# Softmax scaled behind the product with v, weight blocks rounded on ScalarE, and a q held as a rounded pair in a hybrid attention / DeltaNet / RG-LRU trunk

## The chip, the cores and the metric

One core of a Trainium2 chip runs the whole kernel. TensorE (PE; its weight loads are shown as PEld), VectorE (DVE), ScalarE (ACT), GpSimd (POOL) and the DMA queues of SyncE (SP) each run their own list of instructions in order and wait for one another by semaphores. The metric is the device time of one execution in microseconds; three runs gave 2277.67, 2280.9 and 2282.2 us (median 2280.9).

## What is computed

Two layers over 1024 tokens of width 1024, float32. Layer 0 projects x into two head groups: (A) sliding-window attention, 8 query heads on 2 key/value heads of 64, window 128, rotary positions, a learned sink per head; (B) four gated DeltaNet heads of 128. An output projection joins them. Layer 1 is a Griffin recurrent block. Each mixer is followed by a layer norm on `alpha*x + mixer(x)`, then a squared-ReLU MLP of width 4096 and a second layer norm. What the change touches is the attention:

```python
s = jnp.einsum('bnqhgd,bnkhd->bnhgqk', qb, kb) * (DH ** -0.5)      # masked to the window
p = jax.nn.softmax(jnp.concatenate([s, sink], axis=-1), axis=-1)[..., :-1]
o = jnp.einsum('bnhgqk,bnkhd->bnqhgd', p, vb)
```

Dividing each row of exp(s - max) by its sum before the product with v, or dividing the row of the product by it, gives the same o.

## The kernel before

**Halves and streams.** The tokens are cut into two halves of 512 (c = 0 and c = 1). Each half has a stream, a Python generator that runs its projections, MLPs and recurrent blocks: long rows of 128x512 matmuls, "dense work". Beside them run mixers, generators with small steps that wait for other engines: the four attention blocks of a half (`attention`, one `attn_block` per 128 tokens), what goes ahead of them (`attn_preps`: rotary positions, transposes of k and q), the DeltaNet heads (`head_mid`) and the layer norms. State is carried from the first half to the second.

**The order on TensorE.** The order is written while the program is built. `Clock` is a model of the engines; the loop at the end of `trunk` takes a mixer's next step when the model says that its inputs are there, and a step of a stream otherwise, the first half's before the second's while both are in the same phase, the second's first once the first is in its MLP. Each TensorE instruction is tied behind the one before, so that on the chip TensorE follows this order whatever happens. A stream that lacks a resource yields `BLOCK`, and the other is tried. A `UNIT` is the end of a piece, where the loop may change streams.

**Granules and rings.** Large tiles come from a pool of 14 granules of 128x2048 floats (ring "g"), counted by hand: `need("g", n)` blocks a stream until n are free, `gran()` takes one, `free` gives it back. A half's activations (`ActT`) take four: two quads of rows, each as a rounded high part h and the rest l. The attention slots of both halves take two (`slots(8)`: eight tiles of 128x512, `tl`), the residual rows of a mixer's output (`yg` in `mix_out`) two, and `q_proj` one (`st["qg"]`, the projected q of a half, given back when all four `attn_prep` have read it) beside the first quad of the output `oT`. Smaller rings t, s and f hold 128x512 tiles.

**Products in three passes.** Float32 products are made of rounded fp32r parts: `mm3` issues h*h, h*l and l*h. A weight block of 128x1024 is loaded on SP's queue into one of three `ws` buffers (`wblock`); `split` rounds it into `wh`, on VectorE for every fifth block (`HV`) and on ScalarE otherwise, and VectorE subtracts to make `wl`; there are three of each. A block feeds 24 matmuls. Small float32 matmuls are issued directly and show as two records each in the trace, transposes as one.

**The second half's way.** `hybrid(1, ...)` projects one head's k, q and v (`head_front`), the attention's k and v (`kv_proj`), then q (`q`, with `need("g", 3)`), spawns its attention and goes on with the heads; the projection of head 0's z (`head_z`) waits until the first half's `mix_out` has claimed the tiles of its layer norm, and for two granules. The first half's `mix_out` needs two granules before its output projection (`hout`, eight weight blocks) can start, then four for the transposed norm, which it takes over from `oT`.

**Seven products for eight.** Once the second half has made its layer's output projection, a first half's MLP goes over, at an even eighth of the hidden width, from `straight` to `seven`, a Strassen form with 7 products of 24 matmuls in place of 8 per quarter of the second weight matrix.

**An attention block.** `attn_block` makes scores for four pairs of heads (`mx`, from `kT` and qT), masks them and takes the row maximum on VectorE, makes exponentials and row sums `den` on ScalarE, multiplies each of eight 128x256 tiles by its head's 1/den on ScalarE, transposes them on TensorE, copies them from PSUM (VectorE and ScalarE in turn), multiplies by v (`vraw`) into the bank `po`, and splits the result into oT.

Of the kernel before, what the change touches and what calls it, by code (L numbers as in the profile page):

```python
# [17 lines left out]
P = 128  # L18
# [6 lines left out]
GB = 14  # L25
HP = 50
MARGIN = 0.5
WB, WS, HV = 3, 3, 5
RINGS = dict(t=11, s=10, f=4)
FW = 528  # L30
LN_EPS = 1e-5
# [182 lines left out]
def trunk(ctx: ExitStack, tc, I, out):  # L214
# [34 lines left out]
    def gran(dt=F32):  # L249
        return take("g", gpool.tile([P, 2048], dt, tag="g", name=nm("g")))  # L250
# [87 lines left out]
    V.tensor_scalar(rcn, rcs, 4.0, None, ALU.mult)  # L338
    V.tensor_scalar(rcs, rcs, -4.0, None, ALU.mult)

    wcount = [0]

    def split(h, l, x):

        wcount[0] += 1
        (V.tensor_copy if wcount[0] % HV == 0 else S.copy)(h, x)
        V.tensor_tensor(l, x, h, ALU.subtract)

    def wblock(src, n=1024, hl=None):
# [409 lines left out]

    def q_proj(c, x, st, oT):  # L760
        ps = yield from proj_tm([I["hin_q"][i] for i in range(4)], x, 512)
        st["qg"] = gran()
        for n in range(NT):
            oT.quad(0, n)
            S.copy(st["qg"][:, n * CH:(n + 1) * CH], ps[n])
        yield UNIT

    def kv_proj(c, x, st, oT, pre):
        ps = yield from proj_tm([I["hin_kv"][i] for i in range(4)], x, 264, pre=pre)
# [24 lines left out]
        V.tensor_tensor(x4[:, :, :, 1, :], a4[:, :, :, 1, :], b4[:, :, :, 0, :], ALU.add)  # L794

    def attn_prep(c, n, st, tl, o):
        q, kr = v4(st["qg"][:, n * CH:(n + 1) * CH]), st["k"][n]
        yield from need("f", 2)
        a, b, qs = tl[n % 2], ts("f"), v4(ts("f"))
        rope(kr.unsqueeze(1), kr.unsqueeze(1), 1, n, a[:, :128], b[:, :128])  # L800
        rope(qs, q, 4, n, a, b)
        yield at(kr, qs)
        ps = mx_ps()
        PE.transpose(ps[:, :P], kr, ident)
        kT = cpool.tile([P, P], F32, tag="kT", name=nm("kT"), bufs=4)
        V.tensor_copy(kT, ps[:, :P])
        ps = mx_ps()
        for g in range(4):
            PE.transpose(ps[:, g * P:(g + 1) * P], qs[:, g, :], ident)
        free("f", b, qs)  # L810
        S.copy(a, ps)
        o["qT"], o["kT"] = a, kT
        yield at(a, kT)
        o["ok"] = True

    def attn_block(c, n, st, oT, tl, o):
# [34 lines left out]
        S.activation(es, es, AF.Exp)  # L851
        V.tensor_tensor(den, den, es, ALU.add)
        V.reciprocal(den, den)
        for m in (0, 2, 1, 3):
            for g2 in range(2):
                i = 2 * (2 * (m // 2) + g2) + m % 2
                S.activation(pm[m][:, g2, :w], pm[m][:, g2, :w], AF.Copy, scale=den[:, i:i + 1])
        yield at(*pm)
        po = mx_ps()
        pend = None  # L860
# [12 lines left out]
        yield lambda: 0.0  # L873


# [345 lines left out]
    def attn_preps(c, st, o):  # L1221
# [6 lines left out]
        free("g", st["qg"])  # L1228

    def attention(c, st, oT, o):  # L1230
        for n in range(NT):
# [14 lines left out]
    def hybrid(c, x, oT, st, rs):  # L1246
# [21 lines left out]
        for h in range(4):  # L1268
# [235 lines left out]
```

## Time and profile before

| | |
|---|---|
| runs | 2277.67, 2280.9, 2282.2 us; median 2280.9 |
| the profiled execution | 2280.57 us, its span 2278.7 us (1.9 us lie around the span) |
| TensorE busy | 2216.7 us (97%) in 12436 matmuls |
| VectorE, ScalarE busy | 1545.9 us (68%), 1049.1 us (46%) |
| mean granted TensorE clock | 0.991 |

A row of instructions gives line, engine, operation, output <- inputs by the names of the tiles with their numbers left out, shape and count; then busy time and the mean ns of one; then the idle time ahead of them and what ended it. Nearly all rows bear line 178 or 206, the helpers that record every operation, so tiles tell the work apart: `mm` and `mx` are PSUM banks, `g` granules, `wh`, `wl` and `ws` weight blocks, `asc` the small tile with den, `vraw`, `kT`, `kraw` the attention's v and k, `csb` constants with the identity (a matmul from it is a transpose), `S` the DeltaNet state. Matmul ends are modelled: a matmul's own duration is longer than the distance to the next start, so costs are best taken from start to start.

### The profile page before, as it was taken

Reading aid. Unit: us, or ns where it says so; the run is one execution under the profiler, and the core shown is the slowest. Engines: PE = TensorE matmul, PEld = TensorE weight load, DVE = VectorE, ACT = ScalarE, POOL = GpSimd, SP = SyncE. Lnnn points to the kernel's source line nnn. Section 1 sums busy time; section 2 is a strip of 40 time slices with the busy share of each in tenths; the row PEclk is TensorE's granted clock in tenths of the full one; section 3 lists DMA queues with packets and bytes.
Section 4 is the critical chain, followed back from the end, with each engine's and each line's share of the span. In section 5 each row is a group of like instructions: output and inputs, shape, how many; then the busy total and the mean of one; then the engine's idle time right before and its main releaser. Section 6 shows DMA issues by size and latency. Waiting matters only on the chain.

```text
span 2278.7 us, 31897 instructions
## 1 busy us (share of the span) xinstructions
PE 2216.7 (97%) x12436; PEld 1790.4 (79%) x12436; DVE 1545.9 (68%) x2809; ACT 1049.1 (46%) x1874; POOL 28.9 (1%) x56
## 2 busy tenths in 40 slices
PE   8999989999999999999999999999999999999997
PEld 7767866778878887888888878878788887888886
DVE  7787684766645666596567898685565656776477
ACT  5465444434332344454344577373434444444442
POOL 0000000000000000000000000000000000000000
PEclk9999999999999999999999999999999999999999
DMA  4121221266778666677764343322533443454341
GB/s 165 61 78 39 94 67 45 74 175 178 216 213 225 196 211 200 210 241 229 226 216 149 128 138 105 136 79 97 180 107 121 139 148 123 155 166 148 120 163 69
DMA packets 87064, 332.22 MB, mean 146 GB/s; under 512 B 9600, under 2 KB 9984, under 8 KB 78720
## 3 DMA queue, kind: packets, MB, share of 16 engines
q1 hardware_dynamic: 73808, 275.32, 35.2%
q0 software_dynamic: 4608, 33.56, 7.8%
q10 hardware_dynamic: 8496, 21.30, 2.7%
q8 instruction: 97, 1.59, 0.3%
q14 instruction: 55, 0.45, 0.1%
HBM read 321.75 MB, written 75.50 MB: 174 GB/s over the span
## 4 chain that ended last, share of the span: by engine, by line
PE 85%; DVE 9%; ACT 3%; DMA 1%; issue 1%; ACTq 0%; DVEq 0%; SPq 0%
PE mm L206 66%; PE mx L206 17%; DVE g L178 3%; DVE wl L178 2%; PE mx L210 2%; DVE s L178 1%; DMA ws<-w 1%; ACT g L178 1%; ACT wh L178 1%; ACT s L178 1%; DVE t L178 1%; DVE f L178 1%; ACT f L178 0%; ACT t L178 0%; DVE lnw L178 0%
## 5 line engine op out<-in xcount | busy, mean ns | idle before, releaser
L206 PE MATMUL mm<-g,wh 128*128 128x512 f32 x2816 | 883.7, 395 | 3.6 <-DVE g L178 3.0
L178 DVE TENSOR_TENSOR wl<-ws,wh 128x1024 fp32r<-128x1024 f32 (+1 forms) x444 | 538.3, 1212 | 396.1 <-ACT wh L178 391.8
L178 ACT CAST wh<-ws 128x1024 fp32r<-128x1024 f32 (+1 forms) x356 | 371.5, 1044 | 705.8 <-PE mm L206 605.3
L206 PEld LDWEIGHTS mm<-g,wh 128*128 128x128 f32 x2816 | 521.6, 188 | 113.4 <-DVE g L178 5.1
L206 PE MATMUL mm<-g,wl 128*128 128x512 f32 x1408 | 549.5, 390 | 0.5 <-DVE wl L178 0.5
L206 PE MATMUL mm<-wh,s 128*128 128x512 f32 x1152 | 376.6, 393 | 0.7 <-DVE g L178 0.7
L206 PEld LDWEIGHTS mm<-g,wl 128*128 128x128 f32 x1408 | 264.7, 188 | 57.0 <-DVE wl L178 1.0
L206 PEld LDWEIGHTS mm<-wh,s 128*128 128x128 f32 x1152 | 216.3, 188 | 46.7 <-ACT s L178 1.1
L206 PE MATMUL mm<-wh,g 128*128 128x512 f32 (+1 forms) x768 | 239.3, 383 | 6.6 <-ACT wh L178 6.4
L206 PE MATMUL mm<-wl,s 128*128 128x512 f32 x576 | 224.3, 389 | 0.0
L206 PE MATMUL mx<-wh,s 128*128 128x512 f32 x576 | 187.8, 392 | 1.2 <-DVE s L178 1.2
L206 PEld LDWEIGHTS mm<-wh,g 128*128 128x128 f32 x768 | 143.0, 191 | 33.8 <-ACT wh L178 6.4
L178 ACT CAST s<-g 128x512 fp32r<-128x512 f32 x172 | 104.7, 622 | 105.2 <-PE mm L206 53.7
L178 DVE TENSOR_TENSOR s<-g,s 128x512 fp32r<-128x512 f32 x172 | 116.1, 685 | 44.7 <-ACT s L178 44.7
L206 PE MATMUL mm<-wl,g 128*128 128x512 f32 (+1 forms) x384 | 144.1, 375 | 0.2 <-DVE wl L178 0.2
L206 PEld LDWEIGHTS mx<-wh,s 128*128 128x128 f32 x576 | 108.1, 188 | 24.1 <-DVE s L178 2.0
L206 PEld LDWEIGHTS mm<-wl,s 128*128 128x128 f32 x576 | 108.3, 188 | 20.9
L206 PE MATMUL mx<-wl,s 128*128 128x512 f32 x288 | 112.1, 389 | 0.0
L178 DVE CAST wh<-ws 128x1024 fp32r<-128x1024 f32 x88 | 60.4, 686 | 73.0 <-PE mm L206 66.3
L178 DVE TENSOR_TENSOR g<-g,mm 128x512 f32<-128x512 f32 x136 | 89.1, 682 | 14.6 <-PE mm L206 14.2
L178 ACT ACTIVATE g<-mm 128x512 f32<-128x512 f32 x100 | 59.3, 593 | 73.0 <-PE mm L206 73.0
L206 PEld LDWEIGHTS mm<-wl,g 128*128 128x128 f32 x384 | 73.3, 191 | 11.7 <-DVE wl L178 0.6
(231 smaller groups left out, 2401.3 us busy)
## 6 DMA issues: line engine op xcount, KB each, us to landing
ws<-w SPq DMA_DIRECT2D x232, 512.0 KB, 3.3
ws<-t SPq DMA_DIRECT2D x96, 512.0 KB, 3.3
t<-w POOLq DMA_DIRECT2D x32, 1024.0 KB, 9.1
ws<-hin_fm SPq DMA_DIRECT2D x32, 512.0 KB, 3.3
t<-w SPq DMA_DIRECT2D x16, 1024.0 KB, 6.7
t<-t SPq DMA_DIRECT2D x16, 1024.0 KB, 6.5
ws<-rin SPq DMA_DIRECT2D x32, 512.0 KB, 3.3
ws<-hout SPq DMA_DIRECT2D x16, 512.0 KB, 3.4
```

Of the source, the lines that this page charges most:

```text
L178: r = f(*a, **k)
L206: ins = self.pe.matmul(out, lhsT, rhs, start=start, stop=stop, skip_group_check=fresh)
L210: return self._pe(self.pe.transpose(out, x, ident), out, [x], 0.00042 * 2 * out.shape[-1])
```

## The change

Four things. (1) `split` rounds every weight block on ScalarE. (2) In `attn_block` the eight multiplications by 1/den go. Behind the product with v, den (128x8) is transposed on TensorE, copied to `dT` (8x128) by ScalarE, and spread by eight float32 matmuls, each with one column of the identity, repeated 64 times, as the stationary operand, into a 128x512 bank; ScalarE copies that bank to the slot tile `tl[4]`, VectorE multiplies by `po`, and the split into oT reads the slot tile. All copies of transposed scores out of PSUM are made by ScalarE. (3) For the second half, `q_proj` splits q into the parts h and l of oT's first quad and takes no granule of its own; `attn_prep` adds the two parts. `q` then asks for two granules. (4) The `UNIT` at the end of `q_proj` goes, and one is added after a head's `head_mid` is spawned.

```diff
     def split(h, l, x):
-        wcount[0] += 1
-        (V.tensor_copy if wcount[0] % HV == 0 else S.copy)(h, x)
+        S.copy(h, x)
         V.tensor_tensor(l, x, h, ALU.subtract)
...
     def q_proj(c, x, st, oT):
         ps = yield from proj_tm([I["hin_q"][i] for i in range(4)], x, 512)
-        st["qg"] = gran()
+        g = st["qg"] = gran() if c == 0 else None
+        st["q"] = []
         for n in range(NT):
-            oT.quad(0, n)
-            S.copy(st["qg"][:, n * CH:(n + 1) * CH], ps[n])
-        yield UNIT
+            h, l = oT.quad(0, n)
+            if g is None:
+                split_ps(h, l, v4(ps[n]))
+                st["q"].append((h, l))
+            else:
+                S.copy(g[:, n * CH:(n + 1) * CH], ps[n])
+                st["q"].append(v4(g[:, n * CH:(n + 1) * CH]))
...
     def attn_prep(c, n, st, tl, o):
...
         rope(kr.unsqueeze(1), kr.unsqueeze(1), 1, n, a[:, :128], b[:, :128])
+        if c:
+            V.tensor_tensor(qs, *q, ALU.add)
+            q = qs
         rope(qs, q, 4, n, a, b)
...
         V.reciprocal(den, den)
-        for m in (0, 2, 1, 3):
-            for g2 in range(2):
-                i = 2 * (2 * (m // 2) + g2) + m % 2
-                S.activation(pm[m][:, g2, :w], pm[m][:, g2, :w], AF.Copy, scale=den[:, i:i + 1])
         yield at(*pm)
         po = mx_ps()
...
-                (S.copy if h else V.tensor_copy)(pT, ps)
+                S.copy(pT, ps)
                 yield at(pT)
                 PE.matmul(po[h * 64:(h + 1) * 64, :], vv[:, h * 64:(h + 1) * 64], pT, start=(i == 0),
                           stop=(i == len(keys) - 1))
+        yield at(den)
+        ps = mx_ps()
+        PE.transpose(ps[:8, :P], den, ident)
+        dT = cpool.tile([8, P], F32, tag="dT", name=nm("dT"))
+        S.copy(dT, ps[:8, :P])
+        yield at(dT)
+        ps = mx_ps()
+        for i in range(8):
+            g, h = divmod(i, 2)
+            PE.matmul(ps[h * 64:(h + 1) * 64, g * P:(g + 1) * P], ident[0:8, i:i + 1].to_broadcast([8, 64]), dT,
+                      start=True, stop=True)
+        S.copy(tl[4], ps)
+        V.tensor_tensor(tl[4], po, tl[4], ALU.mult)
         h, l = oT.quad(0, n)
-        split_ps(h, l, v4(po))
+        S.copy(h, v4(tl[4]))
+        V.tensor_tensor(l, v4(tl[4]), h, ALU.subtract)
...
         def q():
-            yield from need("g", 3)
+            yield from need("g", 3 - c)
...
             spawn(head_mid(c, h, st, d[h], oT, rs[h % len(rs)]))
+            yield UNIT
```

More of the change, by code (lines that the diff above doesn't have):

```diff
@@ L27 @@
 MARGIN = 0.5
-WB, WS, HV = 3, 3, 5
+WB, WS = 3, 3
 RINGS = dict(t=11, s=10, f=4)
@@ L339, in trunk @@
     V.tensor_scalar(rcs, rcs, -4.0, None, ALU.mult)
-    wcount = [0]
     def split(h, l, x):
-        wcount[0] += 1
-        (V.tensor_copy if wcount[0] % HV == 0 else S.copy)(h, x)
+        S.copy(h, x)
         V.tensor_tensor(l, x, h, ALU.subtract)
@@ L796, in attn_prep @@
     def attn_prep(c, n, st, tl, o):
-        q, kr = v4(st["qg"][:, n * CH:(n + 1) * CH]), st["k"][n]
+        q, kr = st["q"][n], st["k"][n]
         yield from need("f", 2)
@@ L853, in attn_block @@
         V.reciprocal(den, den)
-        for m in (0, 2, 1, 3):
-            for g2 in range(2):
-                i = 2 * (2 * (m // 2) + g2) + m % 2
-                S.activation(pm[m][:, g2, :w], pm[m][:, g2, :w], AF.Copy, scale=den[:, i:i + 1])
         yield at(*pm)
         po = mx_ps()
-        pend = None
         for i, (_, vv) in enumerate(keys):
@@ L1227, in attn_preps @@
             yield from attn_prep(c, n, st, slot["tl"], o[n])
-        free("g", st["qg"])
+        if c == 0:
+            free("g", st["qg"])
     def attention(c, st, oT, o):
```

## The prediction

> **What bounds the kernel now.** I read the page first, then windows, then TensorE's timeline where the windows show it idle. The page says that TensorE is busy 97% of the span. A dense stretch of the chain of waits gives its price: 480 matmuls of 128x512 in 108.94 us, 0.227 us from start to start. Windows (columns: us, then busy us and instruction counts of PE, PEld, DVE, ACT, POOL; granted clock; DMA share; GB/s) show where it isn't full.
>
> ```profile
> PE 2216.7 (97%) x12436; PEld 1790.4 (79%) x12436; DVE 1545.9 (68%) x2809; ACT 1049.1 (46%) x1874; POOL 28.9 (1%) x56
> ...
> 702.00 108.94 PE mm L206 x480
> ...
> 150.00:200.00 50.00, 44.44 (x267) 33.27 (x266) 42.04 (x115) 33.30 (x103) 0.30 (x3) 1.00 0.25 75
> 260.00:317.00 57.00, 55.97 (x399) 46.09 (x401) 46.40 (x158) 29.30 (x98) 0.00 (x0) 1.00 0.26 84
> 317.00:367.00 50.00, 39.05 (x409) 24.02 (x395) 28.31 (x94) 22.75 (x64) 0.00 (x0) 0.80 0.16 54
> 367.00:420.00 53.00, 53.00 (x252) 37.31 (x251) 23.41 (x61) 24.05 (x64) 0.00 (x0) 1.00 0.18 60
> 420.00:470.00 50.00, 46.09 (x219) 37.15 (x220) 47.93 (x117) 26.14 (x58) 0.53 (x1) 0.93 0.27 95
> 1300.00:1450.00 150.00, 147.82 (x658) 121.27 (x657) 131.39 (x205) 101.70 (x157) 0.30 (x3) 0.99 0.40 135
> 1450.00:1600.00 150.00, 144.63 (x644) 118.64 (x643) 100.67 (x157) 79.22 (x116) 0.00 (x0) 0.99 0.27 90
> ```
>
> One stretch stands out: from 317 to 367 us the granted clock is 0.80 and no engine is near full. The timeline of TensorE shows why; the row of SP's queue is from the timeline of all engines.
>
> ```profile
> 316.47 0.39 PE L206 MATMUL mm<-g,wl 128*128 128x512 f32 x1
> 316.79 0.45 PE L206 MATMUL mx<-t 32*32 32x32 f32 x32
> ...
> 356.57 1.07 PE L206 MATMUL mx<-g,vraw 128*64 128x512 f32 x2 [0.41 <-DVE g L178]
> 357.57 0.66 PE L210 MATMUL mx<-csb,g 128*128 128x128 f32 x4
> 358.06 0.61 PE L206 MATMUL mx<-S,t 128*128 128x128 f32 x4
> ...
> 360.54 1.16 PE L206 MATMUL mx<-kT,g 64*128 64x128 f32 x16
> 361.63 0.33 PE L210 MATMUL mx<-csb,kraw 128*128 128x128 f32 x1
> 362.01 0.66 PE L210 MATMUL mx<-csb,f 128*128 128x128 f32 x4
> ...
> 364.96 0.48 PE L206 MATMUL mm<-wh,g 128*128 128x512 f32 x1
> ...
> 371.90 0.39 PE L206 MATMUL mm<-wh,g 128*128 128x512 f32 x1
> 372.13 0.60 PE L206 MATMUL mx<-t,t 128*128 128x128 f32 x4
> 372.49 0.48 PE L206 MATMUL mm<-wh,g 128*128 128x512 f32 x1
> ...
> 306.00 67.64 SPq L178 DMA_DIRECT2D ws<-hout  x4
> ```
>
> Between 316.7 (316.47 + 0.227) and 364.96 us there is no dense matmul at all, only steps of the second half's attention and its first DeltaNet head: a hole of 48.3 us. Dense work is at hand: the loads of `hout`, the first half's output projection, start at 306.00, and that projection starts at 364.96, right behind the transposes of the second half's fourth `attn_prep` (361.63 and 362.01). That is where `qg` is given back. Counting granules in the code at the start of the hole: the first half's oT 4, slots 2, the second half's x 4, its qg 1, its first quad of oT 2. That makes 13 of 14; one is free, and `mix_out` asks for two.
>
> **The change part by part.**
>
> *q in two parts.* Without qg, 12 granules are taken and two are free when the first half's `mix_out` asks. It then starts its output projection before the second half's `head_front` for head 1, which has the dense work up to 316.47. Eight blocks of 24 matmuls (8 x 24 x 0.227 = 43.6 us) become filler for the attention, with their eight loads on SP's queue ahead of three loads of `hin_fm`, and the residual loads on ACT's queue earlier; DMA is busy 0.16 in the hole, so I charge nothing for them; uncovered, one costs the 3.4 us of this row of the page once. The hole's small work must still run. The other groups are of the window 317 to 367:
>
> ```profile
> ws<-hout SPq DMA_DIRECT2D x16, 512.0 KB, 3.4
> ...
> L206 PE MATMUL mx<-g,vraw 128*64 128x512 f32 x16 | 11.3, 794 | 2.6 <-DVE g L178 2.5 <-ACT g L178 0.2
> L210 PE MATMUL mx<-csb,g 128*128 128x128 f32 x32 | 7.2, 349 | 0.9 <-ACT g L178 0.9
> L206 PE MATMUL mx<-kT,g 64*128 64x128 f32 x64 | 4.9, 285 | 0.0
> L206 PE MATMUL mx<-t,t 128*128 128x128 f32 x18 | 4.1, 348 | 1.4 <-DVE t L178 1.3
> L206 PE MATMUL mx<-S,t 128*128 128x128 f32 x16 | 3.6, 364 | 0.0
> L206 PE MATMUL mx<-t 32*32 32x32 f32 x208 | 3.5, 200 | 3.3 <-DVE t L178 2.7 <-DVE kraw L178 0.6
> L206 PE MATMUL mx<-t,t 64*64 64x64 f32 x16 | 2.2, 316 | 2.6 <-DVE asc L178 2.1 <-DVE t L178 0.5
> ```
>
> From start to start in undisturbed places: two `vraw` records 1.00 us (356.57 to 357.57), so 8.0 for 16; four `csb,g` 0.49 (to 358.06), 3.9 for 32; sixteen `kT,g` 1.09 (360.54 to 361.63), 4.4 for 64; four `t,t` between dense matmuls 0.36 (372.13 to 372.49), so 0.09 a record and 3.1 for 34 of `t,t` and `S,t`; the 32x32 groups 0.45 per 32, 2.9; the 64x64 group 2.2 as recorded; two lots of `csb,kraw` and `csb,f` at 0.38 + 0.66, 2.1. Together 26.6 us, some 27. Filling the hole is worth 48.3 - 27 = **21 us**. A part of that comes back: the layer norm now runs earlier, beside two attention blocks, and VectorE is already busy 47.93 of 50 us in its present window, 420 to 470. Dense cover left for it is head 1's `head_front` alone (72 matmuls, 16 us), since `head_z` must wait for the slots' two granules, to the end of the attention. Present waits are these:
>
> ```profile
> 461.92 1.71 PE L210 MATMUL mx<-csb,g 128*128 128x128 f32 x8 [2.25 <-DVE g L178]
> ...
> 465.77 0.79 PE L206 MATMUL mm<-g,wh 128*128 128x512 f32 x1 [1.67 <-DVE g L178]
> ```
>
> 2.25 + 1.67, 4 us. I double them: **+4**, between 0 and the whole 21 (a rival below). The second half's q costs VectorE four subtractions out of PSUM and four additions at 0.68 us, 5.5 us between 230 and 365; it has 10.6 idle us in 260 to 317 alone, and nothing waits on these but the preparation of a block two ahead.
>
> *Softmax behind the product.* These rows bear on it, the first from the timeline of all engines, the others from the groups of the whole span:
>
> ```profile
> 315.36 3.29 ACT L178 ACTIVATE g<-g,asc 128x256 f32<-128x256 f32 x8
> ...
> L178 ACT COPY g<-mx 128x512 f32<-128x512 f32 x23 | 13.5, 586 | 44.0 <-PE mx L210 44.0
> L178 DVE COPY g<-mx 128x512 f32<-128x512 f32 x15 | 10.3, 689 | 16.9 <-PE mx L210 16.9
> L178 DVE TENSOR_TENSOR g<-g,mx 128x512 f32<-128x512 f32 x64 | 41.8, 681 | 0.2 <-PE mx L206 0.2
> ```
>
> 3.29 us a block leave ScalarE, ahead of the transposes. Added per block on TensorE: a transpose (0.38) and 16 records of 128 columns. No row has this shape. Paired like `kT,g` the 16 cost 1.09; at 0.09 each 1.44; at the 0.15 of the isolated `S,t` row (0.61 / 4) 2.4. I take 1.44, the row between dense matmuls, with 0.08 for the re-entry (1.9 in all; bounds 1.2 and 2.8). Four blocks of the second half now lie among dense work and pay in full, 7.6 us. The first half's four lie in stretches like 150 to 200, where TensorE idles 5.6 of 50 us for VectorE: they fall in part into such waits, but TensorE's order is fixed and a wait is filled only by what stands behind it: I charge a quarter, 1.9. Together **+9.5**, between 4.8 (the second half's at 1.2) and 22 (eight at 2.8).
>
> The Trainium skill (TensorE: Matmul & The Clock Gate, Part 3: Packing small matmuls) says that matmuls whose outputs lie in different column groups of the array run side by side, 2.38 times as fast for three. The two heads of a pair write partitions 0 to 63 and 64 to 127, so by it the 16 records would cost about half of 1.44 as an estimate, and the sum would be some 4 us lower; no row here has such a pair back to back, so that stays unshown.
>
> The rest of the tail (a copy of 0.59, the product of 0.68, the split) follows behind TensorE's last step of a block: the next block's scores don't wait for it, and it costs only a longer hold of the bank `po`, one of four. The chain of a block gives up 3.29 us and takes TensorE's 1.8 and the copy to dT, at most 0.59: even. VectorE loses 15 copies (10.3 us) and takes eight products (5.4), ScalarE takes the copies at 0.59: nothing on TensorE's path.
>
> *Rounding on ScalarE.*
>
> ```profile
> L178 ACT CAST wh<-ws 128x1024 fp32r<-128x1024 f32 x349 | 367.1, 1052 | 696.8 <-PE mm L206 596.7 <-PE mx L206 28.7 <-DMA ws<-w 27.6
> L178 DVE CAST wh<-ws 128x1024 fp32r<-128x1024 f32 x87 | 60.0, 689 | 71.9 <-PE mm L206 65.3 <-PE mx L206 4.6 <-DMA ws<-t 1.9
> ```
>
> 87 casts of 0.689 leave VectorE, and as many of 1.052 come to ScalarE: -60 and +92 us. A block feeds 5.4 us of TensorE and three are buffered, so 0.36 us more ahead of `wl` is hidden by two blocks' matmuls. Casts wait for a `wh` buffer (596.7 us), and ScalarE's work behind them waits too; uncovered, that is their mean wait, 1.7 us (596.7/349), a time. At best VectorE's relief pays where it is fullest, 1300 to 1450 (131.39 of 150) and 1450 to 1600, where TensorE idles 2.2 and 5.4 us. I take 0, between -5 and +5. The moved `UNIT` lets the streams change once more per head: 0 too.
>
> *Sum* against the profiled execution's 2280.57 (span 2278.7 and 1.9 around it, 0.3 below the median of the runs, which I neglect): 2280.6 - 21 + 4 + 9.5 = **2273 us**.
>
> **The rivals.**
>
> *Hidden spread.* The new matmuls fall into waits and the layer norm finds cover: 2280.6 - 21 + 4.8 - 3 (relief) = 2261. For it: the 5.6 idle us of 150 to 200. Against it: the second half's four blocks will lie among dense work, where nothing is idle.
>
> *A product lost.* The first half's MLP gains some 10 to 20 us on the second half's heads. If it enters its fifth eighth before the second half's output projection is made, two more eighths run as `straight`, and one quarter pays 8 products for 7: 24 matmuls, 5.4 us. 2273 + 5.4 = 2278. For it: the second half's heads are a chain of small steps that filler can't speed up.
>
> *The hole moves.* With `hout` used up early, the layer norm, slowed on VectorE by the attention, leaves TensorE without dense work for as long as before. The point: it is ready over 21 us after head 1's `head_front` is spent. Then nothing is gained and the spread is paid: 2280.6 + 9.5 = 2290, slower. For it: VectorE's 47.93 of 50. Against it: two attention blocks bring 20 us of small matmuls of their own (by the prices above 8.0 + 3.9 + 4.4, and 3.8 of spread), and the attention's end frees `head_z`.
>
> **How the numbers follow.** Forecast 0.42, hidden spread 0.20, a product lost 0.15, the moved hole 0.23. The likeliest one's own range is 2265 to 2279; cases of both signs are left, so the range is 2257 to 2292. A change under 0.2%, 4.6 us, can't be told from none: faster is below 2276.3 and slower above 2285.5. Forecast gives 0.34 faster and 0.08 the same, hidden spread 0.20 faster, the lost product 0.03 and 0.12, the moved hole 0.02 same and 0.21 slower: 0.57, 0.22, 0.21.
>
> **What would show it.** In the profile after: no stretch of over 10 us without an `mm` matmul between 260 and 370, and clock 1.00 there; `mm<-wh,g` (hout) starting by 275 to 300 rather than at 364.96; eight bursts of 16 records out of `csb` and dT, 1.1 to 2.4 us each; waits for `DVE g` at the layer norm under 10 us; as many `mx<-wh,s` matmuls as now, or 72 fewer `mx` if a product is lost. Wrong would be an output projection that still starts behind the last `attn_prep`, or a stretch without dense work that follows it.

## The result, and the profile after

The changed kernel takes 2300.34 us (median; 2299.26 to 2303.81) against 2280.04 us for the kernel before on the same chip: a ratio of 1.0092, 95% interval 1.0074 to 1.0109. It is 20.3 us slower. The forecast was 2273 us, with a range of 2257 to 2292. The profiled execution took 2299.26 us, its span 2297.4 us, at a mean granted clock of 0.993.

The busy times at the head of the page of the kernel after, and two groups of its whole span:

```profile
PE 2230.2 (97%) x12596; PEld 1798.8 (78%) x12596; DVE 1480.6 (64%) x2707; ACT 1117.0 (49%) x1918; POOL 28.5 (1%) x56
```

```profile
L178 ACT CAST wh<-ws 128x1024 fp32r<-128x1024 f32 x430 | 452.3, 1052 | 753.7 <-PE mm L206 653.6 <-DVE g L178 24.9 <-PE mx L206 21.0
...
L206 PE MATMUL mx<-dT,csb 8*64 8x128 f32 x128 | 8.7, 274 | 0.0
...
L210 PE MATMUL mx<-csb,asc 128*8 128x128 f32 x8 | 2.2, 273 | 0.0
```

TensorE has 160 more matmuls than before (12596 against 12436). The spread explains 128 and the transposes of den 8. The other 24 are one whole weight block: a quarter of the MLP pays 8 products for 7, the case that the prediction had as a rival. VectorE is relieved by 65 us and ScalarE has 68 us more, as the change means; neither is near full.

The windows of the kernel after (us, busy us and counts of PE, PEld, DVE, ACT, POOL, granted clock, DMA share, GB/s), the ones shown of before and some more:

```profile
150.00:200.00 50.00, 47.56 (x259) 36.35 (x258) 44.39 (x122) 35.34 (x106) 0.30 (x3) 0.97 0.25 77
190.00:260.00 70.00, 63.66 (x896) 45.05 (x895) 40.59 (x120) 33.47 (x101) 0.00 (x0) 0.98 0.11 31
260.00:317.00 57.00, 56.03 (x340) 48.51 (x339) 43.67 (x147) 25.34 (x77) 0.00 (x0) 1.00 0.42 137
317.00:367.00 50.00, 48.68 (x504) 33.58 (x503) 28.19 (x80) 20.11 (x52) 0.00 (x0) 1.00 0.17 54
367.00:430.00 63.00, 55.50 (x350) 39.18 (x349) 49.28 (x136) 35.07 (x82) 0.94 (x1) 0.97 0.25 76
420.00:470.00 50.00, 48.52 (x263) 36.24 (x264) 26.11 (x70) 29.07 (x77) 2.56 (x3) 1.00 0.55 153
1300.00:1600.00 300.00, 287.17 (x1271) 235.18 (x1270) 227.64 (x354) 187.76 (x278) 0.40 (x4) 0.98 0.34 111
```

Three of these windows of the kernel before, to set beside them:

```profile
190.00:260.00 70.00, 69.38 (x937) 51.17 (x936) 47.98 (x129) 34.78 (x99) 0.00 (x0) 1.00 0.17 51
...
367.00:430.00 63.00, 63.00 (x293) 44.94 (x292) 31.78 (x74) 25.70 (x66) 0.00 (x0) 1.00 0.18 60
...
1300.00:1600.00 300.00, 292.44 (x1300) 239.91 (x1299) 232.05 (x362) 180.92 (x273) 0.30 (x3) 0.99 0.34 113
```

The old hole is filled: 317 to 367 us went from 39.05 busy us at clock 0.80 to 48.68 at 1.00. But three other stretches got emptier: 190 to 260 by 5.7 us, 367 to 430 by 7.5 us, and 1300 to 1600, far from the attention, by 5.3 us.

The timeline of TensorE after shows that the output projection starts where the prediction wanted it, and that a new stretch without dense work follows (rows of the filled part are left out):

```profile
274.69 0.61 PE L206 MATMUL mm<-wh,g 128*128 128x512 f32 x2
...
413.24 0.40 PE L206 MATMUL mm<-g,wl 128*128 128x512 f32 x1
...
417.23 0.27 PE L210 MATMUL mx<-csb,asc 128*8 128x128 f32 x1
417.85 0.66 PE L210 MATMUL mx<-csb,g 128*128 128x128 f32 x4 [0.35 <-ACT t L178]
418.34 0.61 PE L206 MATMUL mx<-t,t 128*128 128x128 f32 x4
418.88 1.09 PE L206 MATMUL mx<-dT,csb 8*64 8x128 f32 x16
419.90 1.51 PE L206 MATMUL mx<-kT,g 64*128 64x128 f32 x16
...
424.28 0.50 PE L206 MATMUL mm<-g,wh 128*128 128x512 f32 x1
425.68 0.50 PE L206 MATMUL mm<-g,wh 128*128 128x512 f32 x1 [0.89 <-DVE g L178]
```

The projection's first `mm<-wh,g` is at 274.69 instead of 364.96. The first half's MLP, though, starts only at 424.28, behind its layer norm, and from 413.24 to there TensorE has only steps of attention and DeltaNet: 11.0 us. Another such stretch, 17.8 us, lies at 195.86 to 213.65, ahead of the second half's first projection; the kernel before has none there. Such a hole isn't lost in full, since its small work has to run somewhere: TensorE's waits inside the second one add up to 3.1 us.

To see where the 18.7 us of the spans come from, count dense matmuls (128x512 with a rounded weight part) from the end, and note when the one starts behind which N are still to come. The column of before is in us, the others are differences to it, each from the profiled execution; the kernels are those of the experiments below.

```
N to come  before    after  after_     after_x_  layer1_  layer1_      d_scale_
                            product_   product   mixed    mixed_other  behind
                            kept
7680        376.9    -22.8   -35.8      -39.4    -40.3    -41.0          8.8
7440        451.6     10.8     5.8       -0.2     -0.9     -1.9          9.4
6480        728.9      8.7     3.7       -2.3     -3.0     -3.9          9.9
4080       1289.1      9.0     2.3       -3.6     -5.2     -5.0         10.2
3840       1345.3      7.7     0.9       -4.9     -6.6     -4.9         10.3
3600       1405.7     13.9     7.8        2.3     -0.6     -4.9         10.2
3120       1526.8     15.7     6.6        2.6      3.3     -4.9         10.4
   0       2244.5     18.3     7.8        4.1      4.2     -5.0         10.3
```

The kernel after is 22.8 us ahead by this count at 7680 to come, the filled hole, with small work still to be done. It is 10.8 us behind by 7440, past the stretch of the layer norm; 5.4 us of this are the lost product, which runs later but is already among the matmuls to come (after_product_kept, which has as many of them as before, is 5.8 behind). It is 7.7 us behind at 3840, when the first half is in the recurrent blocks of the second layer (layer 1 of the reference). From there on it loses another 10.6 us, 6.2 of them between two rows. So the loss comes in two parts, one in each layer, and the prediction had no term for the second one.

### The profile page after: what moved, and what is told of

Same layout as the page of the kernel before. It is cut to its first block, busy times and chain, and to the rows that moved or that the text cites. A ratio compares the mean times of both kernels' runs of the same rounds, so it can differ in the third digit from the quotient of the medians.

```text
span 2297.4 us, 32236 instructions
## 1 busy us (share of the span) xinstructions
PE 2230.2 (97%) x12596; PEld 1798.8 (78%) x12596; DVE 1480.6 (64%) x2707; ACT 1117.0 (49%) x1918; POOL 28.5 (1%) x56
## 4 chain that ended last, share of the span: by engine, by line
PE 84%; DVE 10%; ACT 4%; DMA 1%; issue 1%; ACTq 0%; DVEq 0%
PE mm L206 65%; PE mx L206 16%; DVE g L178 4%; DVE wl L178 2%; PE mx L210 2%; DVE t L178 1%; ACT g L178 1%; DVE s L178 1%; ACT wh L178 1%; DMA ws<-w 1%; DVE f L178 1%; ACT s L178 1%; ACT t L178 0%; ACT f L178 0%; DVE lnw L178 0%
## 5 line engine op out<-in xcount | busy, mean ns | idle before, releaser
L178 ACT CAST wh<-ws 128x1024 fp32r<-128x1024 f32 (+1 forms) x438 | 457.3, 1044 | 757.2 <-PE mm L206 656.7
L206 PE MATMUL mm<-wh,s 128*128 128x512 f32 x1216 | 398.5, 394 | 5.4 <-DVE g L178 2.8
L206 PEld LDWEIGHTS mm<-wh,s 128*128 128x128 f32 x1216 | 228.3, 188 | 56.1 <-DVE g L178 3.8
L206 PE MATMUL mm<-wl,s 128*128 128x512 f32 x608 | 237.0, 390 | 0.0
L206 PE MATMUL mx<-wh,s 128*128 128x512 f32 x528 | 172.7, 392 | 1.7 <-DVE s L178 1.7
L178 DVE TENSOR_TENSOR s<-g,s 128x512 fp32r<-128x512 f32 x158 | 106.5, 686 | 51.6 <-ACT s L178 51.5
L206 PEld LDWEIGHTS mx<-wh,s 128*128 128x128 f32 x528 | 99.1, 188 | 23.1 <-DVE s L178 3.0
L206 PE MATMUL mx<-wl,s 128*128 128x512 f32 x264 | 102.8, 389 | 0.0
L206 PEld LDWEIGHTS mm<-wl,g 128*128 128x128 f32 x384 | 72.9, 190 | 12.1 <-DVE wl L178 0.5
L206 PE MATMUL mx<-g,wh 128*128 128x512 f32 x256 | 80.7, 397 | 0.0
L210 PEld LDWEIGHTS mx<-csb,g 128*128 128x128 f32 x312 | 36.0, 143 | 38.9 <-issue 15.2
```

The costliest lines, as they stand in the source:

```text
L178: r = f(*a, **k)
L206: ins = self.pe.matmul(out, lhsT, rhs, start=start, stop=stop, skip_group_check=fresh)
L210: return self._pe(self.pe.transpose(out, x, ident), out, [x], 0.00042 * 2 * out.shape[-1])
```

## The experiments

The expectations speak of theories. T1: each part costs what the prediction says, and a lost product comes on top. T2: the work that ScalarE was given (rounding, copies) makes the loss, and q in two parts gains its 17 us. T3: the stall only moves, and q in two parts gains nothing. T4, formed later: the second half's activations come too late. F, H, R and O are explained where they stand. Times are medians; "before" is the kernel before on the same chip. Its medians lie between 2279.2 and 2280.87 us, so that a difference of two runs from different groups is uncertain by some 2 us beside their own spread.

### The parts one by one

*Only q in two parts*, with the smaller need, and without the moved `UNIT` (before 2280.87):

```diff
-        st["qg"] = gran()
+        g = st["qg"] = gran() if c == 0 else None
...
+            if g is None:
+                split_ps(h, l, v4(ps[n]))
...
-            yield from need("g", 3)
+            yield from need("g", 3 - c)
```

> The kernel before with only the second half's q held in two parts (and two granules asked for). Theory 1, three bills: the hole of 48 us is filled (-21), the first half's MLP runs ahead and loses one product (+5.4: the program has 24 more dense matmuls), the layer norm waits a little longer (+4): 2269 us. Theory 2, ScalarE: nothing of ScalarE's new load is here, so nearly the whole gain of the hole is seen: 2264 us or less. Theory 3, the hole only moves to the layer norm behind the output projection: 2280 + 5.4 = 2285 us or more.

Measured: 2284.79 us, ratio 1.0017 [1.0008, 1.0026]. T3's number. The hole of 48 us is gone, and two holes of 10.3 and 18.0 us stand at 359.7 and 373.4 us instead. By the code, the `UNIT` that still ends `q_proj` lets the loop go to the first half's output projection before the second half's attention is spawned, so that the projection is spent before there is anything to hide.

*Only the rounding on ScalarE*:

```diff
-        wcount[0] += 1
-        (V.tensor_copy if wcount[0] % HV == 0 else S.copy)(h, x)
+        S.copy(h, x)
```

> The kernel before with only the weight blocks all rounded on ScalarE. The moved order costs one product here too (24 more dense matmuls). Theory 1: +5.4 and some waits, 2287 to 2290 us. Theory 2: ScalarE's casts are the chief cause, 2294 us or more. Theory 3: 2285 us.

Measured: 2308.04 us, 1.0122 [1.0107, 1.0137], worse than the whole change. It too pays 24 dense matmuls more (8472 for 8448). It has the old hole, 46.1 us at 331.7, and a new one of 17.2 us at 201.8. T2 is nearest; the next group shows that the casts alone don't cost this much.

*Only the scaling behind the product*:

```diff
-                S.activation(pm[m][:, g2, :w], pm[m][:, g2, :w], AF.Copy, scale=den[:, i:i + 1])
...
+            PE.matmul(ps[h * 64:(h + 1) * 64, g * P:(g + 1) * P], ident[0:8, i:i + 1].to_broadcast([8, 64]), dT,
+                      start=True, stop=True)
+        S.copy(tl[4], ps)
+        V.tensor_tensor(tl[4], po, tl[4], ALU.mult)
...
```

> The kernel before with only the softmax scaled behind the product with v (the copies out of PSUM stay in turn on VectorE and ScalarE, no product is lost). Theory 1: eight spreads of 1.02 us and a transpose of 0.2 each in TensorE's list, 2280 + 10 = 2290 us. Theory 2: ScalarE is relieved of 3.3 us a block, which pays for part of it: 2281 to 2285 us. Theory 3 says nothing of it beyond theory 1.

Measured: 2291.36 us, 1.005 [1.0033, 1.0067]. T1's price: +10.5, and the last column above shows that it is nearly all paid by 7440, in the attention, with the second layer as before. That all of it is the spread's own price isn't shown. TensorE is busy 2224.4 us, 7.7 more than before, of the 10.4 us by which the span grew, and one wait is new:

```profile
165.97 1.09 PE L210 MATMUL mx<-csb,t 128*128 128x128 f32 x4 [7.38 <-DVE hsc L178]
```

*Only the copies of transposed scores on ScalarE*:

```diff
-                (S.copy if h else V.tensor_copy)(pT, ps)
+                S.copy(pT, ps)
```

> The kernel before with only the copies of the transposed scores all on ScalarE. Theory 1: ScalarE's order makes the fourth transposes wait, +3: 2283 us. Theory 2: more, 2288 us. Theory 3: no change, 2280 us.

Measured: 2285.76 us, 1.0023 [1.0013, 1.0032], between the two. A part priced at nothing costs 4.9 us by itself. It has a hole of 16.1 us at 196.3, and its window 190 to 260 has 65.10 busy us where before has 69.38.

### Parts put together, and parts taken out

*q in two parts, as above, with the moved `UNIT`* (before 2279.2 here and for the next three):

```diff
-        yield UNIT
...
             spawn(head_mid(c, h, st, d[h], oT, rs[h % len(rs)]))
+            yield UNIT
```

> The kernel before with the second half's q in two parts and the moved UNIT points, so that the second half's attention is spawned before the first half's output projection runs (in b_q_parts it was spawned behind it, and a hole of 25 us of lost time followed from 350 to 400). Theory 1, the hole is filled once the attention starts in time, and only the lost product and 4 us at the layer norm are paid: 2269 us, no stretch of over 10 us without an mm matmul up to 430. Theory 3, the hole moves behind the output projection whichever way: at least 15 us of lost time between 340 and 420, and 2280 to 2287 us.

Measured: 2295.64 us, 1.0075 [1.0058, 1.0092]. Neither. The `UNIT`, priced at 0, moves the time by 10.9 us against b_q_parts (12.5 when each is set against its own before). The holes are now 22.4 us at 205.6 and 16.6 us at 403.0, near the places where the kernel after has its own.

*The kernel after with mixed rounding again*:

```diff
-        S.copy(h, x)
+        wcount[0] += 1
+        (V.tensor_copy if wcount[0] % HV == 0 else S.copy)(h, x)
```

> The changed kernel with every fifth weight block rounded on VectorE again. Theory 2, ScalarE's rounding is the chief cost (21 of the 27 us of a_scalar_rounding beyond its lost product): 2280 us or less. Theory 1: what a_scalar_rounding lost lay in the order that it drew, not in the casts; 2294 to 2300 us.

Measured: 2298.34 us, 1.0081 [1.0066, 1.0096]. T1, and T2 falls as the chief cause: the rounding that cost 27 us alone costs 2.0 us inside the change. This kernel and bc_q_parts_units, on the same chip, differ only in the softmax and its copies. Those cost 10.5 and 4.9 us on the kernel before; here they cost 2.7 together (2298.34 against 2295.64), and the hole behind the projection is 12.6 us at 415.2 instead of 16.6. The parts don't add.

*The kernel after with q in its own granule*, as before:

```diff
-        g = st["qg"] = gran() if c == 0 else None
+        st["qg"] = gran()
...
-            yield from need("g", 3 - c)
+            yield from need("g", 3)
```

> The changed kernel with the second half's q in its own granule again (three granules asked for); no product is lost then. Theory 1: the hole is back, +21 - 4, the product too, -5.4: 2311 us. Theory 3: the hole was only moved, so its return costs nothing and the product's 5.4 us are gained: 2295 us.

Measured: 2298.10 us, 1.0089 [1.0072, 1.0107]. Near T3. The 47.1 us hole is back at 327.0, and yet the time is 2.2 us better than with the hole filled. (The profiled execution took 2306.18 us.) It makes the seven products again, though, so a fair partner is the next run.

*The kernel after with the product kept*, by letting the MLP change over at its fifth eighth when four granules are free:

```diff
-        while e < 8 and not ((c == 1 or sts[1].get("op", -1) >= layer) and rings["g"] >= 2 and e % 2 == 0):
+        while e < 8 and not ((c == 1 or sts[1].get("op", -1) >= layer or e == 4 and rings["g"] >= 4) and rings["g"] >= 2 and e % 2 == 0):
```

> The changed kernel in which the first half's MLP may go over to seven products at its fifth eighth without waiting for the second half's output projection, if four granules are free. All theories: 24 dense matmuls fewer, -5.4: 2295 us, if the order behind it draws no new wait.

Measured: 2291.66 us, 1.005 [1.0035, 1.0065]: 8.7 us better than after. With equal products, q in two parts is worth 2298.10 - 2291.66 = 6.4 us here by the medians of four runs each (8.9 by the ratios 1.0089 and 1.0050), where the prediction had 21 - 4 = 17.

### The two holes

*The second half's loads closer together.* `load_x` waits for four granules and then spaces its four loads by 7 us of the model's time; the second half's stream starts behind them (before 2280.31 here and for the next three):

```diff
-            t = clk.now + 7.0
+            t = clk.now + 1.0
```

> The changed kernel in which the four loads of the second half's x are spaced by 1 us in the plan and not by 7. The traces show no dense matmul from 195.9 for 17.8 us in the changed kernel and none such before; the second half's x, which waits for the granule that the first half's last attn_prep gives back, comes too late there. Theory 4, this second hole is a cost of the change: it goes, 10 to 15 us, 2286 to 2290 us. Theory 3 alone (only the hole at the layer norm counts): it moves on, 2297 to 2300 us.

Measured: 2292.18 us, 1.0057 [1.0042, 1.0072], 8.2 us better than after. The window of this kernel at 190 to 260 us has 3.2 us more of busy TensorE than after:

```profile
190.00:260.00 70.00, 66.86 (x926) 47.78 (x925) 43.96 (x124) 35.74 (x105) 0.00 (x0) 1.00 0.15 47
```

The hole at 196 is gone. The loads of the second half's q, which stood at 230.8 us before and at 250.2 after, start at 230.9. The time is 2.2 us above T4's range and below T3's by 4.8; but T4's reason doesn't hold as far as it speaks of what happens on the chip. Of these rows the first two are from the kernel after, the last loads of the second half's x and the last step of its split, and the other two are the same from this run:

```profile
153.79 10.96 SPq L178 DMA_DIRECT2D ws<-xT  x3
169.53 2.49 DVE L178 TENSOR_TENSOR g<-ws,g 128x512 fp32r<-128x512 f32 x4
...
155.59 11.06 SPq L178 DMA_DIRECT2D ws<-xT  x2
175.05 0.68 DVE L178 TENSOR_TENSOR g<-ws,g 128x512 fp32r<-128x512 f32 x1
```

In the kernel after, x is ready at 172.0 (169.53 + 2.49), 42 us ahead of the projection at 213.65 that reads it; with the closer loads it is ready later, at 175.7, and the hole is gone. So x was late only in the model's time, from which the order is written. A hole near this place is in a_scalar_rounding, d_scale_behind (11.6 us at 202.2), e_scalar_copies, bc_q_parts_units and after_q_granule (18.3 at 195.7) too, and none is in b_q_parts: it isn't q in two parts that draws it, but each of the other parts does. Nor does it always cost something: in d_scale_behind the window 190 to 260 has 69.33 busy us, before 69.38.

*Both*, the closer loads and the changed condition of after_product_kept:

```diff
-            t = clk.now + 7.0
+            t = clk.now + 1.0
```

> The changed kernel with the second half's x sooner and the product kept. Theory 4: the sum of both, 2277 to 2282 us, level with the kernel before. Theory 3 alone: 2289 to 2292 us.

Measured: 2283.92 us, 1.0017 [1.0007, 1.0026], 16.4 us better than after: the two gains of 8.7 and 8.2 add up, nearer T4 than T3.

*The same closer loads in the kernel before*:

```diff
-            t = clk.now + 7.0
+            t = clk.now + 1.0
```

> The kernel before with the second half's x sooner, for comparison. In its trace the second half's first dense work is at hand when the first half's ends, so theory 4 expects little: 2276 to 2283 us.

Measured: 2285.20 us, 1.0023 [1.0014, 1.0032], a loss of 4.9, outside T4's range. So the spacing is no fault by itself: the same edit gains 8.2 us in one kernel and loses 4.9 in the other.

*The kernel after with a lighter layer norm*, without gain and shift in seven of eight pieces of the first layer's first norm:

```diff
-                V.tensor_tensor(a, a, g[i], ALU.mult)
-                V.tensor_tensor(a, a, g[2 + i], ALU.add)
+                if which:
+                    V.tensor_tensor(a, a, g[i], ALU.mult)
+                    V.tensor_tensor(a, a, g[2 + i], ALU.add)
```

> The changed kernel without gain and shift in seven of the eight pieces of the first layer norm of layer 0, which takes 14 x 0.68 = 9.6 us a half off VectorE; its result leaves them out. Theory 3, the filler runs out because the layer norm is slow on VectorE beside the attention: the stretch without dense work at 413 (11 us) shrinks to under 4 us and the time falls by 7 to 12 us, 2289 to 2293 us. If the attention's own chain is what TensorE waits for: under 3 us, 2297 us.

Measured: 2293.68 us, 1.0065 [1.0048, 1.0081], 6.7 us better than after. The hole at 413 is gone and the window is fuller by 4.1 us (59.57 against 55.50):

```profile
367.00:430.00 63.00, 59.57 (x381) 43.78 (x381) 44.75 (x142) 38.65 (x100) 0.94 (x1) 1.00 0.26 76
```

With VectorE's share of the layer norm lighter the hole closes, as the prediction's own rival would have it; the lighter steps change the written order too, and the two aren't told apart.

### Does q in two parts pay once the losses are undone?

F: filling the hole is worth 21 us, and later losses take it. H: it gains nothing, the stall only moves (before 2279.78 here and for the next three).

*Only q in two parts and the moved `UNIT`, with both losses undone* by the closer loads and the condition of after_product_kept; rounding and softmax as before. Of its edit:

```diff
...
-            t = clk.now + 7.0
+            t = clk.now + 1.0
...
-            yield from need("g", 3)
+            yield from need("g", 3 - c)
```

> The kernel before with q in two parts and the moved UNIT, the second half's loads spaced by 1 us in place of 7, and the product kept; softmax and rounding stay as before. F (filling the hole is worth 21 us; three later losses take it): after_x_product without the spread (10 us) and without all rounding on ScalarE (2 us), 2283.9 - 12 = 2272, between 2268 and 2276. H (q in two parts gains nothing even then, the stall only moves): 2280 to 2286.

Measured: 2304.48 us, 1.0108 [1.0095, 1.0122]. Both theories missed. Two windows of this kernel:

```profile
317.00:367.00 50.00, 50.00 (x392) 37.42 (x391) 34.05 (x79) 18.50 (x43) 0.00 (x0) 1.00 0.25 79
367.00:430.00 63.00, 48.21 (x374) 33.50 (x373) 47.15 (x143) 34.85 (x90) 0.94 (x1) 0.88 0.23 64
```

The old hole is full, 50.00 of 50 us, and behind the output projection stands a hole of 35.5 us (393.5 to 429.0): the rival "the hole moves", nearly in full.

*The same with the new softmax*, meant as after_x_product with mixed rounding. The kernel that ran also spaces the loads by 3 us and not by 1, which the expectation doesn't say:

```diff
-        S.copy(h, x)
+        wcount[0] += 1
+        (V.tensor_copy if wcount[0] % HV == 0 else S.copy)(h, x)
...
-            t = clk.now + 1.0
+            t = clk.now + 3.0
```

> after_x_product with every fifth weight block rounded on VectorE again. The mixed rounding gained 2.0 us on the kernel after and its wait of 4.5 us at 1300 to 1450 went: 2282, between 2280 and 2284. If the rounding is worth nothing once the other losses are undone: 2284.

Measured: 2292.48 us, 1.006 [1.0046, 1.0074], 8.6 us more than after_x_product. Two edits lie between them, the rounding and the spacing, and the run can't tell them apart: a hole of 9.6 us stands at 192.8, which after_x_product hasn't, and in the kernel after the spacing alone was worth 8.2 us. So it says nothing firm on the rounding. Against bc_x_product it differs in the softmax, its copies and the spacing: 12.0 us less, with a hole of 12.6 us behind the projection instead of 35.5.

*after_x_product with the lighter norm*:

```diff
-                V.tensor_tensor(a, a, g[i], ALU.mult)
-                V.tensor_tensor(a, a, g[2 + i], ALU.add)
+                if which:
+                    V.tensor_tensor(a, a, g[i], ALU.mult)
+                    V.tensor_tensor(a, a, g[2 + i], ALU.add)
```

> after_x_product, without gain and shift in seven of eight pieces of each half's first layer norm of the first layer (the output leaves these out). If the three losses add up: 2283.9 - 6.6 = 2277.3, between 2275 and 2280. If they share the same time: 2281 to 2284.

Measured: 2284.37 us, 1.0018 [1.0009, 1.0027]: nothing against 2283.92. The hole of 12.1 us at 405.9 is gone and no time with it. The gain of the norm alone shares its time with the other two.

*The lost product alone*, forced on the kernel before:

```diff
-        while e < 8 and not ((c == 1 or sts[1].get("op", -1) >= layer) and rings["g"] >= 2 and e % 2 == 0):
+        while e < 8 and not ((c == 1 or (sts[1].get("op", -1) >= layer and (layer or e >= 6))) and rings["g"] >= 2 and e % 2 == 0):
```

> The kernel before, with the first half's fifth and sixth eighths of the first layer's MLP run one by one, as in the kernel after: 24 dense matmuls more, nothing else. Their own price is 24 x 0.227 = 5.4 us: 2285.7. The run after_product_kept gained 8.7; if the whole of it belongs to the product, 2289.

Measured: 2288.09 us, 1.0032 [1.0021, 1.0044]: +8.3, with an interval of 4.8 to 10.0 that holds both numbers. The 5.4 us of the matmuls and the 8.7 us are not told apart.

### The second layer

In the second layer the change touches only the rounding, and yet it loses 10.6 us there. Rows of the timeline of all engines, the kernel after:

```profile
1377.04 0.62 ACT L178 CAST g<-t 128x512 fp32r<-128x512 f32 x1 [1.61 <-DVE t L178]
1377.57 1.55 ACT L178 CAST g<-mx 128x512 fp32r<-128x512 f32 x3
...
1380.44 0.68 DVE L178 TENSOR_TENSOR g<-mx,g 128x512 fp32r<-128x512 f32 x1
...
1381.18 0.66 PE L210 MATMUL mx<-csb,g 128*128 128x128 f32 x4 [3.94 <-DVE g L178]
```

ScalarE stands 1.61 us at a step of the recurrent block, and behind it in its list are three copies of transposed rows out of PSUM. VectorE subtracts from them only at 1380.44, behind its own steps of the block, and TensorE's next transposes wait 3.94 us. Two runs put the mixed rounding back in the second layer alone (before 2280.37). R: the engine that rounds is the cause; O: the order that comes out is.

```diff
+    rcount = []
     def split(h, l, x):
-        S.copy(h, x)
+        if rcount:
+            rcount[0] += 1
+        (V.tensor_copy if rcount and rcount[0] % 5 == 0 else S.copy)(h, x)
...
+            if not rcount:
+                rcount.append(0)
             ps = yield from proj_fm(I["rin"][4 * b + j], x)
```

> after_x_product, and from the first loads of the second layer on every fifth weight block is rounded on VectorE again; the first layer is untouched. Up to there after_x_product leads the kernel before by 4.9 us and loses 8 to 9 us from there to its end. R (rounding all blocks on ScalarE costs this): 2276 to 2279. O (the order of the steps costs it, whichever engine rounds): the loss only changes by chance, 2280 to 2287.

Measured: 2286.15 us, 1.0026 [1.0017, 1.0036].

```diff
-                rcount.append(0)
+                rcount.append(2)
```

> The same with another choice of the fifth blocks, two earlier in the count. R: the same time as layer1_mixed, within 3 us. O: over 4 us from it.

Measured: 2277.26 us, 0.9985 [0.9976, 0.9994]. The two have the same work on the same engines in the same numbers, and which blocks VectorE takes is worth 8.9 us. TensorE's first 8495 matmuls come in the same order in both traces; from 1328 us on the order differs. That is O: the order alone can cost this much. A window of layer1_mixed, and a wait of it:

```profile
1300.00:1600.00 300.00, 283.39 (x1253) 231.25 (x1252) 225.95 (x350) 176.60 (x264) 0.20 (x2) 0.98 0.33 109
```

```profile
1483.42 1.11 PE L210 MATMUL mx<-csb,g 128*128 128x128 f32 x4 [6.30 <-DVE g L178]
```

The same window of layer1_mixed_other:

```profile
1300.00:1600.00 300.00, 292.45 (x1300) 239.80 (x1299) 228.55 (x354) 180.61 (x272) 0.20 (x2) 0.99 0.34 115
```

One waits 6.30 us for a layer norm's transpose in one place; the other has 292.45 busy us with 1300 matmuls, as the kernel before has (292.44, 1300), and stays 4.9 to 5.0 us ahead of it through the whole layer.

R isn't out of it, though. The count of dense matmuls, made for all the runs, gives what each loses against before from 3840 to come to the end. The eight kernels that round all blocks on ScalarE lose 2.3 (a_scalar_rounding) to 12.6 us, 10.3 in the median; the eleven that share the rounding in this layer lose between -0.8 and 10.8 (layer1_mixed), 1.6 in the median. So rounding on ScalarE goes with a worse order in this layer more often than not, though it doesn't have to, and why it does stays open.

layer1_mixed_other is 3.1 us faster than before, the fastest here. It lies below the 0.2% that the prediction named as the limit of what can be told, though its interval leaves out 1. It isn't the change that was asked about: it has the closer loads, the kept product and another rounding.

## Why the prediction was wrong, step by step

The step that failed is the one from local prices to the whole time. The prediction took the order behind the edited places as it was, and so put at 0 what the edits do to it: the rounding ("0, between -5 and +5"), the moved `UNIT` ("0 too") and the copies ("nothing on TensorE's path"). The runs showed in its place a new order with a price of its own. The `UNIT`, which is no work at all, moved the time by 10.9 us; undoing the lost product, the second half's late start and the second layer's order in the kernel after gave back 8.7, 7.7 and 6.7 us, 23.1 of the 27.3 us between the forecast and 2300.34.

- **The hole of 48.3 us, -21.** The mechanism was right. Two free granules let the output projection start at 274.69, the window went from 39.05 at 0.80 to 48.68 at 1.00. What failed is the step from a filled hole to a shorter time: with equal products the part is worth 6.4 us in the kernel after, and with the old softmax a hole of 35.5 us stands behind the projection.
- **The layer norm, +4.** Undersized. 7.5 us of busy time went at 367 to 430, and the lighter norm got 6.7 us back by itself, though nothing once the other two losses were undone. "Waits for `DVE g` under 10 us" holds for single waits, but the stretch without dense work, which the prediction named as what would prove it wrong, is there, 11.0 us. In the direction of the rival "the hole moves", not in its size.
- **The spread, +9.5.** Right in size, +10.5 alone, and partly by luck: too high a price met too few blocks. A block pays 1.02 us for 16 records (418.88 to 419.90) and 0.27 for the transpose (0.62 less a wait of 0.35), 1.29 in all, where 1.9 was taken; eight of them are 10.3 us. The lower bound of 1.2 left the transpose out (1.09 + 0.38 would be 1.5), and the measured price lies under that too. The forecast let the second half's four blocks pay 7.6 us and the first half's 1.9. In d_scale_behind it is nearer the reverse, 6.5 us with 7800 matmuls to come, when the first half's four bursts are done, and 9.4 at 7440 with all eight; but there the second half's blocks lie in the old hole, so that its share among dense work wasn't tested. The Trainium skill (TensorE: Matmul & The Clock Gate, Part 3: Packing small matmuls) has outputs in different column groups run side by side, and the prediction's sentence on it made that half of 1.44, 0.72 as an estimate. The measured 1.02 lies between: it agrees in direction, if 0.09 us is what such a record costs unpaired, which no run here shows.
- **Copies at nothing.** 4.9 us alone, with a new hole at 196.3. Inside the change they weren't measured apart from the softmax.
- **Rounding on ScalarE, 0, between -5 and +5; the moved `UNIT`, 0.** The argument for 0, that casts are ahead of TensorE, held. A cast still idles 1.52 us for TensorE (653.6/430; before 1.71), and TensorE's own wait for `wh` didn't grow; the first line is before, the second after:

```profile
PE mm L206 <- ACT wh L178: 6.9, 2, 6.4
...
PE mm L206 <- ACT wh L178: 6.5, 1, 6.5
```

  What it left out is that the order of all engines is written from the model's times, so that a changed duration rewrites it. Rounding was worth +27 us alone and +2.0 inside the change, the `UNIT` 10.9.
- **A product lost.** The rival, at 0.15 and 5.4 us, came true, at 8.3 to 8.7 us. The reason was right, as after_product_kept shows: the MLP entered its fifth eighth before the second half's output projection was made. The sign for it was right too: 528 `mx<-wh,s` and 264 `mx<-wl,s` where before has 576 and 288, 72 fewer.
- **Missing: the second half's start.** Its dense work starts late in the written order, though its x is ready, 17.8 us of hole at 196; closing it was worth 8.2 us, of which the window shows 3.2.
- **Missing: the second layer.** 10.6 us in the trace; with the other two losses undone, 6.7 us went with one choice of blocks (2283.92 to 2277.26), and 2.2 came on top with the other (2286.15).

Undone one after the other, the three later losses gave 8.7 us (the product, 2291.66), 7.7 (the second half's start, 2283.92) and 6.7 (the second layer, 2277.26). The first two gave 8.7 and 8.2 each by itself, so they add; the third was undone only on top of them, by the better of two choices. Each of these edits writes a new order too, and a neutral choice alone moved the time by 8.9 us, so that how much of each gain is the named cause and how much the luck of the order isn't shown; for the product, its own 24 matmuls explain 5.4 of the 8.7. What is left is 3.1 us under before. If the forecast's 21 are won and 10.5 paid for the spread, 7.4 are left for the stretch of the layer norm and the rest, by subtraction and not by a run.

What stays open is which single step of the order makes each of these differences. Why the hole behind the projection is shorter with the new softmax, which adds work to TensorE (16.6 and 12.6 us in the pair that differs in nothing else), wasn't settled. A chain of the attention that no longer has ScalarE's eight multiplications would do it; that is argued, not shown.

## What to carry to other kernels

Where the program writes its instruction order from a model of the engines, an edit has two costs: its own work, which the rows price within their bounds (a spread: 1.2 to 2.8 us forecast, 1.29 measured), and a new order for everything behind it, which no row of the old trace prices. Here the two together came to 5 to 27 us for edits that had been priced at 0, so a range of 2257 to 2292 built from local bounds was too narrow. Before crediting a filled hole, write down what the stream that filled it does next and when its input is ready; and when a mechanism depends on who gets somewhere first (a fifth eighth, a granule), check each such race anew, in the written order as well as on the chip. Trying a neutral setting (which blocks VectorE rounds) in two versions shows how far the order alone moves the time: 8.9 us here.

## What the chip showed that was not expected

Sixteen records of eight 8x64 by 128 matmuls, in pairs that write partitions 0 to 63 and 64 to 127, took 1.02 us from start to start: 64 ns a record, against the 0.09 us of the 128x128 records among dense matmuls that the prediction used. Three bursts of the kernel after (at 210.76, 243.00 and 418.88) took the same 1.02 us. The prediction had a nearer row: sixteen `kT,g` records in 1.09 us, 68 ns each.
